# Order of products in a two-layer trunk: joint and third products by sixteens, and the end of the convolution

## The chip, the cores and the metric

The kernel runs on one core of a Trainium2 chip. Its time is the device time of one execution in microseconds, as the median of three runs. Times of parts come from one profiled execution of the kernel before.

## The reference

Two layers over 256 tokens of width 1024, in float32. Each layer is a half-step feed-forward block (SwiGLU, hidden width 2816), a token mixer, and another half-step feed-forward block, with RMS norms ahead of and behind each. The first layer's mixer is a convolution module, the second's a gated linear recurrence (HGRN2).

```python
def swiglu_ffn(x, w_in, w_out):
    gate, up = jnp.split(x @ w_in, 2, axis=-1)
    return (jax.nn.silu(gate) * up) @ w_out

def conformer_conv_module(x, w_in, b_in, w_dw, b_dw, ln_g, ln_b, w_out, b_out):
    a, gate = jnp.split(x @ w_in + b_in, 2, axis=-1)
    h = a * jax.nn.sigmoid(gate)
    h = lax.conv_general_dilated(  # 31 taps, causal, each channel by itself
        ...
    h = jax.nn.silu(layer_norm(h, ln_g, ln_b))
    return h @ w_out + b_out

for layer in range(DEPTH):
    ...
    x = x + 0.5 * rms_norm(h, g[1])
    hn = rms_norm(x, g[2])
    ...
```

## The kernel before

**Three products for one.** Float32 values are split into a high part (a cast to float32r, on ScalarE, L136) and the rest (a subtraction on VectorE, L137); `split` does both. A product of two such values is the sum of three: high by high, high by rest, rest by high. `mm3` (L140 to L142) issues the three.

**Tokens.** The 256 tokens are two tiles t = 0, 1 of 128. `xhl` holds the transposed input of the current block for both tiles, high and rest side by side.

**Feed-forward blocks.** There are four, each with 11 chunks of 256 hidden columns. Chunk 0 is done by tiles (`up`, `turn`), chunks 1 to 10 by `up_both(c, b)` for b = 0, 1, each of which calls `channels` once: 20 calls a block, 80 in all. `channels` computes 128 gate channels and 128 up channels for all tokens. A part (gate in a PSUM bank of the pool `mm`, up in one of `tr`, two banks in each pool) is eight joint products, the weight's high part by high and rest of `xhl` together (512 columns, L331), then eight third products, the weight's rest by the high part (256 columns, L333). A copy of the cross half and an add (L336, L337) read the bank. Behind two calls of `up_both` come the products of `down` of the chunk before (L140 to L142 into `acc`).

**The convolution, `conv_mixer`.** The channels lie in four chunks c of 256, so there are eight pairs (t, c). `gate(t, c)` projects (`project`, L291 to L295), adds the bias, and splits the gated value into `glu`. `conv(t, c)` takes it through a discrete Fourier transform: 6 or 12 small products into `tr` (L140 to L142 there), a complex multiplication by the taps' spectrum on VectorE (L513 to L517), a split into `yh`, `yl` (`cc` in the trace), six products back into another `tr` bank, the bias (L526) and the statistics of the layer norm (L527). `norm(t)` combines the statistics, takes the power on GpSimd (L151, L155) and makes z (L536). `turn(t, z)` transposes z in two halves of four blocks (L546), applies gain and bias by block on ScalarE (L553), then sigmoid (L557), multiplication (L558) and split into `xhl`: by pairs of blocks in the first half, all four at once in the second. `expand` multiplies the result by the output weights `wo` (48 products a tile), and `post_norm` (L267 to L279) adds it to x. What is returned as `rest` is run by the next block, ahead of its own norms (`start`, `pre_norm`, whose transposes are L175).

**What sets the order.** The kernel is written in Tile. Its scheduler fills the engines' queues at build time: of the instructions that by its own estimate of times are ready, the one written first goes first. What is written earlier is thus preferred, not fixed. On the chip each engine runs its queue in that order. `behind(engine)` keeps what is written under it behind the last instruction written for that engine. Banks and buffers of a pool are given in the order of use. Weights come on SyncE's queue (`weight`, L127) and are split as they land.

The convolution's written order is gate and conv for (0,0), (1,0), (0,1), (1,1), (0,2), (0,3); norm(0); gate and conv (1,2); gate(1,3); turn(0); conv(1,3); loads of rows and of `wo`; norm(1) and turn(1); expand(0) and post_norm(0).

Of the kernel before, what the change touches and what calls it, by code (L numbers as in the profile page):

```python
# [11 lines left out]
AF = mybir.ActivationFunctionType  # L12
ALU = mybir.AluOpType
# [27 lines left out]
def trunk_kernel(  # L41
# [39 lines left out]
    def acc():  # L81
        return new(ps, [P, 512], F32, "acc", 4)

    def mm():
        return new(ps, [P, 512], F32, "mm", 2)

    def tr():
        return new(ps, [P, 512], F32, "tr", 2)
# [46 lines left out]
    def split(dst_h, dst_l, src):  # L135
        act.copy(dst_h, src)  # L136
        dve.tensor_tensor(dst_l, src, dst_h.bitcast(F32), op=ALU.subtract)  # L137
# [185 lines left out]

    def channels(ws, cols_, scales):
        res = wide("ga")
        for part, bank in enumerate((mm, tr)):
            o = bank()
            pair = o.rearrange("p (s t m) -> p s t m", s=2, m=P)
            block = lambda w, k: w[:, (k % 2) * 512 + cols_[part] : (k % 2) * 512 + cols_[part] + P]
            for k in range(KD):  # L330
                pe.matmul(pair, block(ws[k // 2][0], k), xhl[:, k], start=k == 0, stop=False)  # L331
            for k in range(KD):
                pe.matmul(pair[:, 0], block(ws[k // 2][1], k), xhl[:, k, 0],  # L333
                          start=False, stop=k == KD - 1)
            cross = narrow("e")
            act.copy(cross, o[:, SEQ:])  # L336
            dve.tensor_tensor(res[:, part * SEQ : (part + 1) * SEQ], o[:, :SEQ], cross, op=ALU.add)  # L337
        dve.tensor_tensor(res[:, :SEQ], res[:, :SEQ], scales, op=ALU.mult)
        return res
# [131 lines left out]
    def conv_mixer(layer, spectrum, before):  # L471
# [4 lines left out]
        xt = start(base, before)  # L476
        hc = [b4() for _ in range(NT)]
        stats = [new(sb, [P, 4, 6], F32, "stats", 2) for _ in range(NT)]
        glu = {}
        ws = {}  # L480

        def gate(t, c):
# [12 lines left out]
            split(hl[:, :CH], hl[:, CH:], h)  # L495
            glu[t, c] = hl

        def conv(t, c):
            sl = slice(c * CH, (c + 1) * CH)
            u = tr()  # L500
            srcs = [(glu[t, c], C_FWD)]
            if t > 0:
# [8 lines left out]
            m1, m2 = wide("ca"), wide("cb")  # L511
            y = m1
            dve.tensor_tensor(m1[:NH], u[:NH, :], wri, op=ALU.mult)  # L513
            dve.tensor_tensor(m2[:NH, :CH], u[:NH, :CH], wi, op=ALU.mult)
            dve.tensor_tensor(m2[:NH, CH:], u[:NH, CH:], wr, op=ALU.mult)
            dve.tensor_tensor(y[:NH, :CH], m1[:NH, :CH], m1[:NH, CH:], op=ALU.subtract)
            dve.tensor_tensor(y[:NH, CH:], m2[:NH, :CH], m2[:NH, CH:], op=ALU.add)  # L517
            yh, yl = wide("cc", F32R), wide("cc", F32R)
            split(yh[:NH], yl[:NH], y[:NH])
            v = tr()  # L520
            for part in range(2):
                cs = slice(C_INV + part * P, C_INV + (part + 1) * P)
# [6 lines left out]
        def norm(t):  # L529
            mv = tiny(2)  # L530
            dve.bn_aggr(mv, stats[t])
            rstd = rsqrt(mv[:, 1:2], 1.0, EPS)
            z = b4()
            for n in range(2):
                sl = slice(n * 512, (n + 1) * 512)
                dve.tensor_scalar(z[:, sl], hc[t][:, sl], mv[:, 0:1], rstd,  # L536
                                  op0=ALU.subtract, op1=ALU.mult)
            return z

        def turn(t, z):  # L540
            hi, lo = turned(t)
            for h in range(2):
                pt = tr()
                for j in range(4):
                    k = h * 4 + j
                    pe.transpose(pt[:, j * P : (j + 1) * P], z[:, k * P : (k + 1) * P], ident)  # L546
                y, s = hc[t][:, h * 512 : (h + 1) * 512], z[:, h * 512 : (h + 1) * 512]
                for j in range(4):
                    k = h * 4 + j
                    js = slice(j * P, (j + 1) * P)  # L550
                    g = gcol[:, G_LN + k : G_LN + k + 1]
                    b = gcol[:, G_LN + KD + k : G_LN + KD + k + 1]
                    act.activation(y[:, js], pt[:, js], AF.Identity, scale=g, bias=b)  # L553
                step = 256 if h == 0 else 512
                for a in range(0, 512, step):
                    bs = slice(a, a + step)
                    act.activation(s[:, bs], y[:, bs], AF.Sigmoid)  # L557
                    dve.tensor_tensor(y[:, bs], y[:, bs], s[:, bs], op=ALU.mult)  # L558
                    ks = slice((h * 512 + a) // P, (h * 512 + a + step) // P)
                    split(hi[:, ks], lo[:, ks], y[:, bs].rearrange("p (k m) -> p k m", m=P))  # L560
            return hi, lo

        for t, c in ((0, 0), (1, 0), (0, 1), (1, 1), (0, 2)):
            gate(t, c)
            conv(t, c)
        gate(0, 3)
        conv(0, 3)
        za = norm(0)
        gate(1, 2)
        conv(1, 2)  # L570
        gate(1, 3)
        sa = turn(0, za)
        conv(1, 3)
        b_out = row(V_BOUT)
        gain = row(V_POST + base)
        wo = [weight(True) for _ in range(8)]
        sbt = turn(1, norm(1))
        accs = [[acc(), acc()] for _ in range(NT)]
        expand(accs[0], blocks(*sa, KD), wo, True, True)
        post_norm(0, accs[0], gain, 1.0, b_out)  # L580

# [361 lines left out]
```

## Time and profile before

| | |
|---|---|
| median of 3 runs | 1009.26 us (1008.78 to 1009.34) |
| profiled execution | 1008.88 us |
| its span, first to last instruction | 1007.0 us |
| mean granted TensorE clock | 0.995 |
| TensorE busy | 992.5 us |
| VectorE busy | 749.7 us |
| ScalarE busy | 548.6 us |

A row of a timeline is: start, duration, engine, line, operation, output<-inputs by the program's names, shapes, count; in square brackets idle time of the engine before it and what ended it. Products are pipelined, so durations overlap: what a product costs is the distance from its start to the next start. [...]

### The profile page before, as it was taken

The page shows a single profiled execution, that of the slowest core. Times are in us where ns is not written, and L with a number is a line of the kernel's source. Part 1 is how long each engine was busy: PE and PEld are TensorE (multiplying, and loading weights), DVE is VectorE, ACT ScalarE, POOL GpSimd, SP SyncE. Part 2 cuts the span into 40 slices and gives each one's busy share as a digit, 9 for nine tenths or more (in the row PEclk, how much of TensorE's full clock was granted, in tenths as well). Part 3 has the DMA queues.
Part 4 walks back from the last instruction along what each step waited for, and adds up shares of the span by engine and source line. Part 5 has one row for each costly group of instructions (what it writes and reads, how often), then busy time and mean ns, then how long its engine had stood idle before and what let it go on. Part 6 is the DMA issues. An engine that isn't in the chain of part 4 may idle for free.

```text
span 1007.0 us, 14787 instructions
## 1 busy us (share of the span) xinstructions
PE 992.5 (99%) x5412; PEld 854.8 (85%) x5412; DVE 749.7 (74%) x1274; ACT 548.6 (54%) x1000; POOL 53.6 (5%) x93
## 2 busy tenths in 40 slices
PE   9999999999899999999999999999999999999997
PEld 7888888888778888888888888889998888888886
DVE  6877667799887776767776767687788596767673
ACT  6656545764485555455755554584143385555541
POOL 1000000010021000000200000030001120000000
PEclk9999999999899999999999999999999999999999
DMA  7885555642527564646465646465232555555541
GB/s 250 273 279 181 187 198 172 236 179 104 181 96 235 180 219 161 222 160 221 168 198 178 210 166 223 167 208 179 82 126 93 179 195 181 189 187 199 178 147 42
DMA packets 50952, 182.06 MB, mean 181 GB/s; under 512 B 6048, under 2 KB 6176, under 8 KB 50880
## 3 DMA queue, kind: packets, MB, share of 16 engines
q1 hardware_dynamic: 50736, 181.09, 53.4%
q8 instruction: 42, 0.69, 0.3%
q14 instruction: 30, 0.25, 0.1%
q10 hardware_dynamic: 144, 0.03, 0.0%
HBM read 180.06 MB, written 1.05 MB: 180 GB/s over the span
## 4 chain that ended last, share of the span: by engine, by line
PE 94%; DVE 2%; ACT 1%; DMA 1%; POOL 1%; issue 0%; DVEq 0%; POOLq 0%; SPq 0%; ACTq 0%
PE tr L331 14%; PE mm L331 14%; PE acc L141 9%; PE acc L140 9%; PE acc L142 9%; PE tr L333 7%; PE mm L333 7%; PE mm L291 4%; PE mm L292 4%; PE mm L295 4%; PE tr L654 2%; PE mm L351 2%; PE mm L352 2%; PE mm L350 2%; DMA raw<-wts 1%; PE tr L175 1%
## 5 line engine op out<-in xcount | busy, mean ns | idle before, releaser
L137 DVE TENSOR_TENSOR wl<-raw,wh 128x1024 fp32r<-128x1024 f32 (+1 forms) x386 | 399.9, 1059 | 89.1 <-ACT wh L136 65.0
L136 ACT CAST wh<-raw 128x1024 fp32r<-128x1024 f32 (+1 forms) x386 | 340.4, 921 | 124.7 <-DMA raw<-wts 72.3
L331 PE MATMUL mm<-xt,wh 128*128 128x512 f32 x640 | 161.6, 393 | 0.5 <-ACT wh L136 0.5
L331 PE MATMUL tr<-xt,wh 128*128 128x512 f32 x640 | 160.7, 392 | 0.0
L140 PE MATMUL acc<-wh,b 128*128 128x512 f32 x352 | 138.0, 392 | 0.0
L141 PE MATMUL acc<-wl,b 128*128 128x512 f32 x352 | 137.4, 390 | 0.0
L331 PEld LDWEIGHTS mm<-xt,wh 128*128 128x128 f32 x640 | 116.9, 188 | 24.1 <-ACT wh L136 1.3
L142 PE MATMUL acc<-wh,b 128*128 128x512 f32 x352 | 137.0, 389 | 0.0
L331 PEld LDWEIGHTS tr<-xt,wh 128*128 128x128 f32 x640 | 115.0, 189 | 20.7
L333 PEld LDWEIGHTS mm<-xt,wl 128*128 128x128 f32 x640 | 87.5, 190 | 6.7 <-DVE wl L137 0.4
L333 PEld LDWEIGHTS tr<-xt,wl 128*128 128x128 f32 x640 | 87.3, 190 | 6.2
L333 PE MATMUL mm<-xt,wl 128*128 128x256 f32 x640 | 90.0, 282 | 0.2 <-DVE wl L137 0.2
L333 PE MATMUL tr<-xt,wl 128*128 128x256 f32 x640 | 89.2, 282 | 0.0
L136 ACT CAST b<-e 128x256 fp32r<-128x256 f32 x80 | 32.5, 406 | 95.8 <-DVE e L412 95.8
L142 PEld LDWEIGHTS acc<-wh,b 128*128 128x128 f32 x352 | 66.1, 188 | 14.1
L140 PEld LDWEIGHTS acc<-wh,b 128*128 128x128 f32 x352 | 66.2, 188 | 12.6
L141 PEld LDWEIGHTS acc<-wl,b 128*128 128x128 f32 x352 | 66.2, 188 | 12.2
L336 ACT COPY e<-tr 128x256 f32<-128x256 f32 x80 | 29.4, 368 | 85.1 <-PE tr L333 85.1
L337 DVE TENSOR_TENSOR ga<-tr,e 128x256 f32<-128x256 f32 x80 | 33.7, 421 | 55.6 <-ACT e L336 55.6
L291 PE MATMUL mm<-wh,xt 128*128 128x512 f32 x176 | 70.0, 398 | 0.0
L292 PE MATMUL mm<-wl,xt 128*128 128x512 f32 x176 | 69.2, 393 | 0.0
L336 ACT COPY e<-mm 128x256 f32<-128x256 f32 x80 | 29.7, 371 | 49.0 <-PE mm L333 48.8
(180 smaller groups left out, 1251.9 us busy)
## 6 DMA issues: line engine op xcount, KB each, us to landing
raw<-wts SPq DMA_DIRECT2D x328, 512.0 KB, 4.8
b<-rows SPq DMA_DIRECT2D x10, 512.0 KB, 6.5
b<-x_turned SPq DMA_DIRECT2D x4, 256.0 KB, 6.3
x<-x_in SPq DMA_DIRECT2D x2, 512.0 KB, 8.4
out_dram<-x SPq DMA_DIRECT2D x4, 256.0 KB, 2.0
b<-dft SPq DMA_DIRECT2D x1, 371.0 KB, 4.8
ca<-masks SPq DMA_DIRECT2D x1, 192.0 KB, 4.5
b<-w_dw SPq DMA_DIRECT2D x1, 128.0 KB, 4.9
```

The source lines that it names most:

```text
L136: act.copy(dst_h, src)
L137: dve.tensor_tensor(dst_l, src, dst_h.bitcast(F32), op=ALU.subtract)
L140: pe.matmul(o, lh, rh, start=first, stop=False)
L141: pe.matmul(o, lh, rl, start=False, stop=False)
L142: pe.matmul(o, ll, rh, start=False, stop=last)
L291: pe.matmul(o, hi[:, k], wh[:, sl], start=k == 0, stop=False)
L292: pe.matmul(o, hi[:, k], wl[:, sl], start=False, stop=False)
L295: pe.matmul(o, a, w, start=False, stop=h == 1 and n == 3)
L331: pe.matmul(pair, block(ws[k // 2][0], k), xhl[:, k], start=k == 0, stop=False)
L333: pe.matmul(pair[:, 0], block(ws[k // 2][1], k), xhl[:, k, 0], start=False, stop=k == KD - 1)
L336: act.copy(cross, o[:, SEQ:])
L337: dve.tensor_tensor(res[:, part * SEQ : (part + 1) * SEQ], o[:, :SEQ], cross, op=ALU.add)
```

## The change

In `channels` the four groups of eight products are issued in another order: joint products of gate, joint of up, third of gate, third of up. Both banks are taken at the start, and both are read at the end.

In `conv_mixer`, `conv` is cut in two, `spectral` (up to the split) and `back` (the six products back, bias, statistics). For (1,2), `back` is written behind gate(1,3) and turn(0). Of the two multiplications by half of the spectrum's swapped parts one of 512 columns is made, which reads the spectrum with its halves exchanged. In `turn`, gain and bias, sigmoid, multiplication and split go by pairs of blocks in both halves. turn(1) gets the bank `accs[1][0]` as `spare`: behind its last transposes 16 products of the identity by itself are written into it, whose result nobody reads. The accumulators are taken ahead of turn(1) for that.

```diff
--- before.py
+++ after.py
@@ -323,15 +323,18 @@
 
     def channels(ws, cols_, scales):
         res = wide("ga")
-        for part, bank in enumerate((mm, tr)):
-            o = bank()
+        banks = [mm(), tr()]
+        for o, col in zip(banks, cols_):
             pair = o.rearrange("p (s t m) -> p s t m", s=2, m=P)
-            block = lambda w, k: w[:, (k % 2) * 512 + cols_[part] : (k % 2) * 512 + cols_[part] + P]
             for k in range(KD):
-                pe.matmul(pair, block(ws[k // 2][0], k), xhl[:, k], start=k == 0, stop=False)
+                wh = ws[k // 2][0][:, (k % 2) * 512 + col : (k % 2) * 512 + col + P]
+                pe.matmul(pair, wh, xhl[:, k], start=k == 0, stop=False)
+        for o, col in zip(banks, cols_):
+            pair = o.rearrange("p (s t m) -> p s t m", s=2, m=P)
             for k in range(KD):
-                pe.matmul(pair[:, 0], block(ws[k // 2][1], k), xhl[:, k, 0],
-                          start=False, stop=k == KD - 1)
+                wl = ws[k // 2][1][:, (k % 2) * 512 + col : (k % 2) * 512 + col + P]
+                pe.matmul(pair[:, 0], wl, xhl[:, k, 0], start=False, stop=k == KD - 1)
+        for part, o in enumerate(banks):
             cross = narrow("e")
             act.copy(cross, o[:, SEQ:])
             dve.tensor_tensor(res[:, part * SEQ : (part + 1) * SEQ], o[:, :SEQ], cross, op=ALU.add)
@@ -476,7 +479,7 @@
         xt = start(base, before)
         hc = [b4() for _ in range(NT)]
         stats = [new(sb, [P, 4, 6], F32, "stats", 2) for _ in range(NT)]
-        glu = {}
+        glu, prod = {}, {}
         ws = {}
 
         def gate(t, c):
@@ -495,8 +498,7 @@
             split(hl[:, :CH], hl[:, CH:], h)
             glu[t, c] = hl
 
-        def conv(t, c):
-            sl = slice(c * CH, (c + 1) * CH)
+        def spectral(t, c):
             u = tr()
             srcs = [(glu[t, c], C_FWD)]
             if t > 0:
@@ -511,12 +513,18 @@
             m1, m2 = wide("ca"), wide("cb")
             y = m1
             dve.tensor_tensor(m1[:NH], u[:NH, :], wri, op=ALU.mult)
-            dve.tensor_tensor(m2[:NH, :CH], u[:NH, :CH], wi, op=ALU.mult)
-            dve.tensor_tensor(m2[:NH, CH:], u[:NH, CH:], wr, op=ALU.mult)
+            dve.tensor_tensor(m2[:NH].rearrange("p (s n) -> p s n", s=2),
+                              u[:NH].rearrange("p (s n) -> p s n", s=2),
+                              wri.rearrange("p (s n) -> p s n", s=2)[:, ::-1, :], op=ALU.mult)
             dve.tensor_tensor(y[:NH, :CH], m1[:NH, :CH], m1[:NH, CH:], op=ALU.subtract)
             dve.tensor_tensor(y[:NH, CH:], m2[:NH, :CH], m2[:NH, CH:], op=ALU.add)
             yh, yl = wide("cc", F32R), wide("cc", F32R)
             split(yh[:NH], yl[:NH], y[:NH])
+            prod[t, c] = yh, yl
+
+        def back(t, c):
+            yh, yl = prod.pop((t, c))
+            sl = slice(c * CH, (c + 1) * CH)
             v = tr()
             for part in range(2):
                 cs = slice(C_INV + part * P, C_INV + (part + 1) * P)
@@ -537,45 +545,49 @@
                                   op0=ALU.subtract, op1=ALU.mult)
             return z
 
-        def turn(t, z):
+        def turn(t, z, spare=None):
             hi, lo = turned(t)
             for h in range(2):
                 pt = tr()
                 for j in range(4):
                     k = h * 4 + j
                     pe.transpose(pt[:, j * P : (j + 1) * P], z[:, k * P : (k + 1) * P], ident)
+                if spare is not None and h == 1:
+                    with behind(pe):
+                        for j in range(16):
+                            pe.matmul(spare[:, j % 4 * P : (j % 4 + 1) * P], ident, ident, start=True, stop=True)
                 y, s = hc[t][:, h * 512 : (h + 1) * 512], z[:, h * 512 : (h + 1) * 512]
-                for j in range(4):
-                    k = h * 4 + j
-                    js = slice(j * P, (j + 1) * P)
-                    g = gcol[:, G_LN + k : G_LN + k + 1]
-                    b = gcol[:, G_LN + KD + k : G_LN + KD + k + 1]
-                    act.activation(y[:, js], pt[:, js], AF.Identity, scale=g, bias=b)
-                step = 256 if h == 0 else 512
-                for a in range(0, 512, step):
-                    bs = slice(a, a + step)
+                for a in range(0, 512, 256):
+                    bs = slice(a, a + 256)
+                    ks = slice((h * 512 + a) // P, (h * 512 + a + 256) // P)
+                    for j in range(a // P, a // P + 2):
+                        k = h * 4 + j
+                        js = slice(j * P, (j + 1) * P)
+                        g = gcol[:, G_LN + k : G_LN + k + 1]
+                        b = gcol[:, G_LN + KD + k : G_LN + KD + k + 1]
+                        act.activation(y[:, js], pt[:, js], AF.Identity, scale=g, bias=b)
                     act.activation(s[:, bs], y[:, bs], AF.Sigmoid)
                     dve.tensor_tensor(y[:, bs], y[:, bs], s[:, bs], op=ALU.mult)
-                    ks = slice((h * 512 + a) // P, (h * 512 + a + step) // P)
                     split(hi[:, ks], lo[:, ks], y[:, bs].rearrange("p (k m) -> p k m", m=P))
             return hi, lo
 
-        for t, c in ((0, 0), (1, 0), (0, 1), (1, 1), (0, 2)):
+        for t, c in ((0, 0), (1, 0), (0, 1), (1, 1), (0, 2), (0, 3)):
             gate(t, c)
-            conv(t, c)
-        gate(0, 3)
-        conv(0, 3)
+            spectral(t, c)
+            back(t, c)
         za = norm(0)
         gate(1, 2)
-        conv(1, 2)
+        spectral(1, 2)
         gate(1, 3)
         sa = turn(0, za)
-        conv(1, 3)
+        back(1, 2)
+        spectral(1, 3)
+        back(1, 3)
         b_out = row(V_BOUT)
         gain = row(V_POST + base)
         wo = [weight(True) for _ in range(8)]
-        sbt = turn(1, norm(1))
         accs = [[acc(), acc()] for _ in range(NT)]
+        sbt = turn(1, norm(1), accs[1][0])
         expand(accs[0], blocks(*sa, KD), wo, True, True)
         post_norm(0, accs[0], gain, 1.0, b_out)
```

## Rows read from the trace of the kernel before

**Rows 1.** The page's first part: busy time and share of the span of TensorE.
```profile
PE 992.5 (99%) x5412; PEld 854.8 (85%) x5412; DVE 749.7 (74%) x1274; ACT 548.6 (54%) x1000; POOL 53.6 (5%) x93
```

**Rows 2.** Windows: stretch, length, busy PE, PEld, DVE, ACT, POOL, clock, DMA.
```profile
256.00:281.00 25.00, 20.80 (x95) 16.80 (x94) 20.10 (x44) 14.25 (x35) 0.74 (x2) 0.86 0.43 158
...
300.00:1000.00 700.00, 700.00 (x3916) 609.51 (x3915) 509.43 (x824) 366.97 (x638) 35.20 (x57) 1.00 0.53 176
```

**Rows 3.** TensorE's waits: sum, count, longest.
```profile
PE tr L140 <- ACT cc L136: 2.7, 1, 2.7
...
PE tr L175 <- DVE x L279: 1.2, 2, 0.6
```

**Rows 4.** Timeline of TensorE in a chunk of the second feed-forward block.
```profile
323.11 1.98 PE L331 MATMUL mm<-xt,wh 128*128 128x512 f32 x8
324.92 1.12 PE L333 MATMUL mm<-xt,wl 128*128 128x256 f32 x8
325.88 2.00 PE L331 MATMUL tr<-xt,wh 128*128 128x512 f32 x8
327.72 1.12 PE L333 MATMUL tr<-xt,wl 128*128 128x256 f32 x8
328.67 2.00 PE L331 MATMUL mm<-xt,wh 128*128 128x512 f32 x8
```

**Rows 5.** Timeline of TensorE at the convolution's end.
```profile
255.44 1.08 PE L295 MATMUL mm<-wh,xt 128*128 128x512 f32 x4
259.24 0.39 PE L140 MATMUL tr<-cc,b 81*128 81x256 f32 x1 [2.72 <-ACT cc L136]
259.46 0.66 PE L546 MATMUL tr<-ident,b 128*128 128x128 f32 x4
...
276.67 1.11 PE L546 MATMUL tr<-ident,b 128*128 128x128 f32 x8 [0.29 <-DVE b L536]
277.54 0.47 PE L140 MATMUL acc<-wh,xt 128*128 128x512 f32 x1
...
278.77 0.40 PE L142 MATMUL acc<-wh,xt 128*128 128x512 f32 x1
280.18 0.50 PE L140 MATMUL acc<-wh,xt 128*128 128x512 f32 x1 [1.01 <-ACT xt L136]
```

**Rows 6.** Windows of 2 us at the convolution's end.
```profile
258.00:260.00 2.00, 0.77 (x5) 0.59 (x5) 2.00 (x6) 1.33 (x3) 0.00 (x0) 0.97 0.61 248
260.00:262.00 2.00, 1.82 (x8) 1.43 (x8) 1.41 (x5) 1.85 (x6) 0.00 (x0) 0.50 0.00 0
...
266.00:268.00 2.00, 2.00 (x9) 1.60 (x8) 2.00 (x6) 1.74 (x4) 0.00 (x0) 0.82 0.51 168
```

**Rows 7.** The page's groups: busy us, mean ns, idle before.
```profile
L337 DVE TENSOR_TENSOR ga<-tr,e 128x256 f32<-128x256 f32 x80 | 33.7, 421 | 55.6 <-ACT e L336 55.6
```

**Rows 8.** Timeline of TensorE early in the first feed-forward block.
```profile
41.27 0.50 PE L333 MATMUL mm<-xt,wl 128*128 128x256 f32 x2 [0.23 <-DVE wl L137]
```

**Rows 9.** Timeline of VectorE at the convolution's end.
```profile
254.31 1.01 DVE L536 TENSOR_SCALAR b<-b,tiny,tiny 128x512 f32<-128x512 f32 x2 [0.71 <-POOL tiny L155]
...
255.83 0.68 DVE L513 TENSOR_TENSOR ca<-tr,b 81x512 f32<-81x512 f32 x1
256.43 0.41 DVE L514 TENSOR_TENSOR cb<-tr,b 81x256 f32<-81x256 f32 x1
256.76 0.41 DVE L515 TENSOR_TENSOR cb<-tr,b 81x256 f32<-81x256 f32 x1
...
276.07 1.00 DVE L536 TENSOR_SCALAR b<-b,tiny,tiny 128x512 f32<-128x512 f32 x2 [0.95 <-POOL tiny L155]
```

**Rows 10.** Waits from 256 to 286: VectorE's for TensorE.
```profile
DVE b L526 <- PE tr L142: 1.9, 2, 1.3
...
DVE ca L513 <- PE tr L142: 0.6, 1, 0.6
```

**Rows 11.** Timeline of TensorE at the kernel's start.
```profile
1.50 5.49 PE L202 MATMUL tr<-ident 128*128 128x128 f32 x24 [1.50 <-POOL ident masks.py:199]
```

## The prediction

> **What bounds the kernel now.** I read the page's first part, then the windows by stage, TensorE's waits, and the timelines of the two places that the change touches. TensorE is busy for 992.5 of 1007.0 us and no other engine is near that [rows 1]. In the windows the 700 us after the convolution have no idle time at all on TensorE at a granted clock of 1.00, while the 25 us at the convolution's end (256 to 281) have 20.80 busy and a clock of 0.86 [rows 2]. So time can go only in two ways: make the stream of products itself shorter, or close what is lost at the convolution's end. The list of waits agrees: the longest is 2.7 us, a product `tr<-cc` that waits for a split on ScalarE; two waits of transposes for `x`, up to 0.6 each, stand a little behind [rows 3].
>
> **The lost time, added up.** Product starts in the timeline [rows 5] give it. The last four products of gate(1,3) start at 255.44, 0.23 apart, so the next could start at 256.35; it starts at 259.24: 2.9 lost. Later pauses are 0.29 and 1.01 [rows 5] and one of the two of 0.6 [rows 3], each with 0.15 or so around it for the pipeline to refill (from 278.77 to 280.18 are 1.41, a product's spacing of 0.23 and the wait of 1.01 leave 0.17): 2.4 together. [...] Two us by the missing shares is 2 x (0.03 + 0.5 + 0.5 + 0.5 + 0.18) = 3.4 us. Sum: 2.9 + 2.4 + 3.4 = 8.7 us. It is all that the convolution part can win.
>
> **Part 1, `channels`.** It removes and adds no product: 8 joint (512 columns), 8 third (256), 8 joint, 8 third become 16 joint, 16 third. The price lies at the seams. Joint eights that follow other 512-column products take 1.81 us (323.11 to 324.92); those that follow thirds take 1.84 (325.88 to 327.72) [rows 4]. Thirds take 0.95 to 0.96 an eight, 0.12 each. The change takes one seam third-to-joint out of each call: 0.03 us. It also takes one joint-to-third seam out, which gains nothing or gives back up to 0.01, the rounding of the rows. There are 80 calls (x80) [rows 7]. So 80 x 0.02 = 1.6 us less; by rounding between 0.8 and 2.8. The third products now come 1.8 us after the last joint of their own bank, so `wl` has that much longer: the wait of 0.23 at 41.27, 0.4 with the refill [rows 8], should go; I take 0.3. Joint products need all four `wh` as soon as before, so waits for `wh` stay.
>
> What it moves: both banks now fill almost together, and the `mm` bank is read 2.8 us later. The work on each bank ends with an add of 0.42 [rows 7] behind a copy of like size; the same bank is asked for two calls later, and a call lasts 5.56 us (323.11 to 328.67) [rows 4]. That is the cover, and it is wide; without it each of 80 calls would wait. At the end of a feed-forward block the chain after the last third product still ends with the `tr` half, so no change there.
>
> **Part 2, the order at the convolution's end.** TensorE takes instructions in queue order, and that order isn't the written one: products of expand(0), written last, stand on both sides of turn(1)'s transposes (`acc<-wh,xt` goes on at 277.54) [rows 5]. Written order works as a priority among what the scheduler deems ready. Before, the inverse products of conv(1,2) have priority over turn(0); the first one waits until 259.24 for `yh`, and turn(0)'s transposes, whose `z` was done at 255.32 [rows 9], wait behind it until 259.46. The reason that `yh` is late is on VectorE: it idles 0.71 for GpSimd's power, then does `z`, and only from 255.83 the products of conv(1,2) [rows 9]. Told ahead of back(1,2), the transposes can start at about 256.4, 3.0 us earlier (their bank was last used by conv(0,3)). So turn(0)'s activations and splits, and with them expand(0), come up to 3 us earlier.
>
> What is late next? (a) TensorE between 256.4 and 260 has only eight transposes (0.9 us) and six inverse products (0.7): I take 2.0 us of pause as left, bounds 0.5 and 2.9. (b) VectorE: from 255.83 to 277.07, the end of z(1), it idles 1.9 (two waits for the inverse products), 0.6 and 0.95 = 3.45 [rows 9, 10], so some 17.8 us of work lie ahead of z(1), the splits of `wo` among it. z(1) can't end before 273.6 unless splits go behind it; 0.95 for GpSimd remains; so 274.6, which is 2.5 us earlier. TensorE has, until turn(1), 48 products of expand(0) at 0.227, 24 small ones of the convolution at 0.12 and 8 transposes at 0.11 [rows 4, 5]: 10.9 + 2.9 + 0.9 = 14.7 us, so with the pause of 2.0 from 256.35 to about 273. The two fit: TensorE is through with expand(0) shortly before z(1) is there. (c) the combined multiplication: two of 256 lie 0.33 apart and one of 512 takes 0.60 to the next [rows 9], so 0.06 less in each of 8 blocks, only the last on the path. Two halves instead of one 512 in turn's second part cost the same 0.06 or so for each multiplication and split, and let the first half go on sooner. I count all of (c) as nothing.
>
> [...]
>
> **Part 3, identity products.** [...] Sixteen make 32 instructions: 3.5 us by the near row in form and clock, 7.3 by the other, which is the bound; I take 3.5. They stand behind the last transposes of turn(1) and ahead of whatever of expand(0) isn't issued yet. The pause they are to fill is, before, from 277.54 to 280.18, 2.6 us, of which six products of expand(0) take 1.4 and 1.01 is seen as idle. If expand(0) is through by then, 2.6 us of 3.5 are covered; if not, they delay it. Either way I charge all 3.5 against the removal of the whole pause. They write `accs[1][0]`, which nobody needs before expand(1).
>
> **Sum of parts 2 and 3.** 8.7 are lost now; after: 2.0 pause at 256 to 260, 3.5 identity products in place of the last pause, 0.7 for the smaller waits that stay (z(1), `x`). Left 6.2, so 2.5 less. This takes the clock as held. With part 1: 2.5 + 1.6 + 0.3 = 4.4 us. The profiled execution took 1008.88 (its span 1007.0 and 1.88 around it), so 1004.5; the median of the runs is 0.38 above it, so **1004.9 us**. Bounds of the unknown costs around it: 1.5 either way for the pause, 1.0 for the seams, so about 1002.4 to 1007.4.
>
> **Rivals.**
> *The clock falls anyway.* For it: it fell about where the pause before 259.24 ended, and in the change the same stretch holds only short work, mostly transposes. Against it: the transposes and the inverse products break the pause, where before it was whole [rows 5]. Price: the 3.4 us stay, and 1004.9 + 3.4 = 1008.3, no measurable change. [...]
> *Slower: the identity products run with real work queued behind them at half clock.* It decides if the clock is still down when turn(1) is transposed. Then they take 7 us rather than 3.5, on top of the case above: 1008.3 + 3.5 = 1011.8. Against it: the stretch at half clock ended before 268 [rows 6], well ahead of 276.67 [rows 5].
> *It doesn't do what it says.* The scheduler places by its own estimate; if back(1,2) still goes ahead, part 2 gives nothing and the products cost 3.5 less the 1.2 of the pause: 1009.26 - 1.9 + 2.3 = 1009.7.
> *More than forecast.* Both pauses shrink to 0.5 and the identity products fit into a pause that the chain through z(1) leaves anyway: 1.5 and 1.8 more, 1001.6.
>
> **How the numbers follow.** Forecast 0.55, clock falls 0.15, slower 0.08, order unchanged 0.08, more 0.14. A change of 0.2%, 2.0 us, is about what a measurement of this kernel can tell from none. Faster by more: the forecast and the larger gain, 0.69, and a little of the clock's case, in all 0.70; within: 0.20; slower: 0.10. The range, 1001.2 to 1009.2, takes in all but the slower case and the edges of the others.
>
> **What would show it.** In the changed trace: joint sixteens of about 3.63 to 3.66 us and third sixteens of 1.91; turn(0)'s first transposes at about 256.4 rather than 259.46 and ahead of the inverse products; a clock of 1.00 from 256 to 281; 32 identity instructions 0.11 apart, with at most 0.3 us of pause behind them; the transposes of `x` for the next block (285.1 before) some 2.5 us earlier in that stage. I am wrong if the seams don't shrink, if the clock is 0.50 again around 260, or if the identity products stand ahead of many products of expand(0).

## The result, and the profile after

The changed kernel is slower. Its median is 1021.09 us (1020.51 to 1021.63), that of the kernel before, run beside it, 1009.30 (1008.78 to 1010.73): a ratio of 1.0113, 95% interval 1.0100 to 1.0126, or 11.8 us more. The forecast was 1004.9, the range 1001.2 to 1009.2; sign and range are wrong. The profiled execution of the changed kernel took 1020.51 us, its span is 1018.7.

The windows of the kernel after say where (columns as in [rows 2]):

```profile
256.00:281.00 25.00, 13.24 (x70) 11.61 (x69) 19.36 (x44) 14.65 (x39) 0.74 (x2) 0.66 0.48 165
...
306.00:1006.00 700.00, 699.16 (x3919) 609.42 (x3918) 507.12 (x826) 372.67 (x649) 35.13 (x60) 1.00 0.52 175
```

The 700 us behind the convolution are all but as full as before, 699.16 us of work against 700.00 [rows 2]. In the 25 us at its end TensorE worked 13.24 us where it had worked 20.80 [rows 2], at a clock of 0.66 for 0.86. The timeline of TensorE in that stretch, kernel after; the rows with brackets are pieces of work that begin behind a pause:

```profile
256.94 1.04 PE L554 MATMUL tr<-ident,b 128*128 128x128 f32 x8
260.67 0.39 PE L140 MATMUL tr<-cc,b 81*128 81x256 f32 x1 [2.69 <-ACT b L568]
...
262.98 0.50 PE L140 MATMUL tr<-lg,b 128*81 128x256 f32 x1 [1.34 <-ACT b L568]
...
269.46 0.58 PE L140 MATMUL tr<-cc,b 81*128 81x256 f32 x1 [3.63 <-ACT cc L136]
...
275.58 1.94 PE L554 MATMUL tr<-ident,b 128*128 128x128 f32 x8 [3.53 <-DVE b L544]
277.31 4.65 PE L558 MATMUL acc<-ident 128*128 128x128 f32 x32
281.71 0.48 PE L140 MATMUL acc<-wh,xt 128*128 128x512 f32 x1
...
296.44 1.38 PE L175 MATMUL tr<-ident,x 128*128 128x128 f32 x8 [0.18 <-DVE x L279]
```

The first line is the early start of turn(0) as forecast: its eight transposes in one piece at 256.94, where their first half had come at 259.46 [rows 5]. What is missing is `acc<-wh,xt`: before, 42 of the 48 products of expand(0) ran ahead of turn(1)'s transposes; now not one does. The first stands at 281.71, behind the identity products. With nothing to run beside the convolution's chain TensorE waits 2.69, 1.34, 3.63 and 3.53 us. The clock is down with it (windows of 4 us, the clock is the third number from the end):

```profile
260.00:264.00 4.00, 1.99 (x11) 1.79 (x12) 4.00 (x12) 4.00 (x13) 0.00 (x0) 0.77 0.39 144
...
268.00:272.00 4.00, 1.97 (x6) 1.43 (x6) 4.00 (x8) 0.62 (x1) 0.00 (x0) 0.50 0.46 148
...
276.00:280.00 4.00, 4.00 (x24) 4.00 (x23) 1.19 (x3) 3.30 (x10) 0.00 (x0) 0.60 0.36 139
```

It fell to 0.50 at about 262.2 and rose at 279.2, 17 us against 6.8 before.

**The account.** From turn(1)'s transposes to those of `x` it is 296.44 - 275.58 = 20.86 us after. Before, from 276.67 [rows 5] to this row of the same timeline, it was 8.45:

```profile
285.12 0.66 PE L175 MATMUL tr<-ident,x 128*128 128x128 f32 x4 [0.57 <-DVE x L279]
```

Between them stand 63 products of the expansions rather than 24: 39 x 0.227 = 8.9. The identity products take 281.71 - 277.31 = 4.4, the transposes at half clock 277.31 - 275.58 = 1.73 rather than 0.87, so 0.9 more. The pause of 1.01 with its refill is gone (-1.2) and the wait for `x` is 0.4 shorter. Together 12.6; measured 12.4. turn(1) came 1.1 us earlier (0.8 of it from before the convolution), which leaves 11.3 at the transposes of `x`. The rest is small: +0.9 from there to the second feed-forward block, where 33 products of the expansions are left rather than 30 (0.7), -0.4 in each of the three blocks that follow, +0.6 between two of them. That makes the 11.7 by which the span grew.

**Part 1 did what it said, block by block.** Timeline of a chunk, kernel after:

```profile
335.31 1.98 PE L331 MATMUL mm<-xt,wh 128*128 128x512 f32 x8
337.12 1.98 PE L331 MATMUL tr<-xt,wh 128*128 128x512 f32 x8
338.93 1.11 PE L336 MATMUL mm<-xt,wl 128*128 128x256 f32 x8
339.88 1.12 PE L336 MATMUL tr<-xt,wl 128*128 128x256 f32 x8
340.84 0.40 PE L331 MATMUL mm<-xt,wh 128*128 128x512 f32 x1
```

Sixteen joint products take 338.93 - 335.31 = 3.62, sixteen third products 1.91, a call 5.53 where it was 5.56 [rows 4]. The first joint product of a block and the first product behind its last call, before and then after:

```profile
491.14 0.48 PE L331 MATMUL mm<-xt,wh 128*128 128x512 f32 x1
...
649.85 0.40 PE L140 MATMUL acc<-wh,b 128*128 128x512 f32 x1
```
```profile
503.61 0.48 PE L331 MATMUL mm<-xt,wh 128*128 128x512 f32 x1
...
661.93 0.40 PE L140 MATMUL acc<-wh,b 128*128 128x512 f32 x1
```

158.71 us became 158.32. The wait for `wl` of [rows 8] is gone.

### The profile page after: what moved, and what is told of

Read it like the earlier page. It is cut to its first block, busy times and chain, and to the rows that moved or that the text cites. A ratio compares the mean times of both kernels' runs of the same rounds, so it can differ in the third digit from the quotient of the medians.

```text
span 1018.7 us, 14830 instructions
## 1 busy us (share of the span) xinstructions
PE 996.0 (98%) x5444; PEld 859.6 (84%) x5444; DVE 746.6 (73%) x1270; ACT 552.4 (54%) x1004; POOL 49.1 (5%) x93
## 4 chain that ended last, share of the span: by engine, by line
PE 93%; DVE 3%; ACT 2%; DMA 1%; POOL 1%; issue 0%; DVEq 0%; POOLq 0%; SPq 0%; ACTq 0%
PE mm L331 14%; PE tr L331 14%; PE acc L141 9%; PE acc L140 9%; PE acc L142 9%; PE mm L336 7%; PE tr L336 7%; PE mm L295 4%; PE mm L292 4%; PE mm L291 4%; PE tr L666 2%; PE mm L354 2%; PE mm L355 2%; PE mm L353 2%; DVE wl L137 1%; DMA raw<-wts 1%
## 5 line engine op out<-in xcount | busy, mean ns | idle before, releaser
L331 PE MATMUL tr<-xt,wh 128*128 128x512 f32 x640 | 158.6, 390 | 0.0
L331 PEld LDWEIGHTS tr<-xt,wh 128*128 128x128 f32 x640 | 119.8, 188 | 25.3 <-DVE ga L340 0.4
L336 PEld LDWEIGHTS tr<-xt,wl 128*128 128x128 f32 x640 | 82.8, 192 | 0.3
L140 PEld LDWEIGHTS acc<-wh,b 128*128 128x128 f32 x352 | 66.2, 188 | 12.6
L340 DVE TENSOR_TENSOR ga<-mm,e 128x256 f32<-128x256 f32 x80 | 33.6, 420 | 52.4 <-ACT e L339 52.4
L413 ACT ACTIVATE e<-ga 128x256 f32<-128x256 f32 x80 | 33.5, 419 | 57.9 <-DVE ga L341 56.1
```

The lines of the kernel that those rows point to most:

```text
L140: pe.matmul(o, lh, rh, start=first, stop=False)
L331: pe.matmul(pair, wh, xhl[:, k], start=k == 0, stop=False)
L336: pe.matmul(pair[:, 0], wl, xhl[:, k, 0], start=False, stop=k == KD - 1)
L413: act.activation(h, gu[:, :SEQ], AF.Sigmoid)
```

## The experiments

Theory: the identity products, as the first in the kernel's text to write a bank of `acc`, decide the order in which the banks of that pool are handed out; the scheduler then can't queue expand(0), written behind them in the same pool, before them, and they stand behind turn(1). Rivals: the time of the identity products themselves; the new order of turn(0) and back(1,2); the clock. "Told" stands for written in the kernel's text. Ratios are against the kernel before, run in the same group.

| kernel | median us (runs) | before | ratio, 95% interval |
|---|---|---|---|
| e1_no_identity | 1008.70 (11) | 1009.82 | 0.9984, 0.9976 to 0.9993 |
| e2_channels_only | 1010.27 (11) | 1009.82 | 1.0003, 0.9995 to 1.0012 |
| e3_identity_only | 1024.07 (4) | 1009.82 | 1.0131, 1.0116 to 1.0146 |
| e4_identity_in_mm | 1010.16 (12) | 1009.82 | 1.0003, 0.9993 to 1.0013 |
| e6_one_identity | 1019.05 (4) | 1009.95 | 1.0085, 1.0072 to 1.0098 |
| e7_expand_told_first | 1009.37 (10) | 1009.95 | 0.9996, 0.9987 to 1.0005 |
| e11_turn_in_mm | 1007.06 (5) | 1009.95 | 0.9965, 0.9953 to 0.9977 |
| e11b_turn_in_mm, the same again | 1007.13 (9) | 1009.67 | 0.9973, 0.9963 to 0.9982 |
| e13_identity_first_pause | 1007.49 (8) | 1009.95 | 0.9977, 0.9967 to 0.9988 |
| e10_back_early | 1009.60 (11) | 1010.16 | 0.9997, 0.9988 to 1.0005 |
| e12_turn_in_mm_expand_first | 1008.23 (11) | 1010.16 | 0.9984, 0.9975 to 0.9993 |
| e16_old_channels_e12 | 1008.40 (11) | 1010.16 | 0.9984, 0.9975 to 0.9993 |
| e14_identity_first_pause_mm | 1007.49 (7) | 1010.16 | 0.9973, 0.9962 to 0.9983 |
| e18_joint_third_by_twos | 1007.73 (11) | 1009.67 | 0.9981, 0.9972 to 0.9990 |
| e15_old_channels_e11 | 1007.63 (11) | 1009.67 | 0.9979, 0.9970 to 0.9987 |

### Who makes it slow: the identity products, and by their bank

**e1** leaves the identity products out of the changed kernel; the accumulators are still taken ahead of turn(1).

```diff
-        sbt = turn(1, norm(1), accs[1][0])
+        sbt = turn(1, norm(1))
```

> The changed kernel (1021.1) without the sixteen identity products, all else kept. Theory A (the identities take the first bank of the pool acc, which the scheduler hands out in order of first writing in the text, so the 48 products of expand(0) can't be queued ahead of them): expand(0) is back ahead of turn(1), 44 of its 48 products; 1005 to 1007. Theory B (the new order of back(1,2) and turn(0) is itself the loss, through the banks of tr and ScalarE): 1015 or more. Theory C (only the time of the 32 identity instructions at half clock, 4.7 us, and nothing else): 1021.1 - 4.7 = 1016.4.

**e3** puts them alone into the kernel before, by the same lines in its `turn`.

```diff
-        sbt = turn(1, norm(1))
         accs = [[acc(), acc()] for _ in range(NT)]
+        sbt = turn(1, norm(1), accs[1][0])
```

> The kernel before with the identity products alone, into accs[1][0], and the accumulators taken ahead of turn(1). Theory A: expand(0) falls behind turn(1) here too, 42 products of 0.227 (9.5 us) lose their place beside the chain through VectorE and the clock falls for longer: 1019 to 1023. Theory B: only the products' own time, 3.5 less the pause of 1.2: 1011.6. Theory C: 1009.3 + 4.7 = 1014.

**e4** is the changed kernel with the same 32 instructions in a bank of another pool.

```diff
-        sbt = turn(1, norm(1), accs[1][0])
+        sbt = turn(1, norm(1), mm())
```

> The changed kernel with the sixteen identity products written into a bank of the pool mm rather than accs[1][0]; same number, same place behind the last transposes of turn(1). Theory A: expand(0) comes back ahead of turn(1) (44 of 48), the identities cost at most 3.5 less what of the last pause they fill: 1006 to 1009. Theories B and C: as the changed kernel, 1020 to 1022.

e1 is 1.1 us faster than the kernel before where the changed kernel is 11.8 slower, e3 is 14.3 slower, and e4, with every identity product still there and still behind turn(1)'s transposes, is level with it. In e1 44 of the 48 products of expand(0) are back ahead of turn(1), in e4 too; in e3 none is, although its turn(0), its back(1,2) and its `channels` are those of before. TensorE in e3, behind a pause that the kernel before has as 0.29 [rows 5]:

```profile
276.32 1.97 PE L546 MATMUL tr<-ident,b 128*128 128x128 f32 x8 [3.43 <-DVE b L536]
278.09 5.52 PE L550 MATMUL acc<-ident 128*128 128x128 f32 x32
283.36 0.48 PE L140 MATMUL acc<-wh,xt 128*128 128x512 f32 x1
```

In e4 the identity products stand at the same place, and expand(0) goes on around them:

```profile
276.48 0.39 PE L141 MATMUL acc<-wl,xt 128*128 128x512 f32 x1
277.23 1.06 PE L554 MATMUL tr<-ident,b 128*128 128x128 f32 x8 [0.36 <-DVE b L544]
278.13 3.74 PE L558 MATMUL mm<-ident 128*128 128x128 f32 x32
281.62 0.48 PE L142 MATMUL acc<-wh,xt 128*128 128x512 f32 x1
```

So the new order at the convolution's end isn't the cause, and neither is the identity products' own time in the main: it is the bank.

**e6** keeps one identity product of sixteen, in the same bank, and **e7** keeps all and the bank, but tells expand(0) ahead of turn(1), so that it is the first to write `acc`.

```diff
-                        for j in range(16):
+                        for j in range(1):
```

> The changed kernel with one identity product instead of sixteen, still written into accs[1][0] behind turn(1)'s last transposes. Theory A (the order of the acc banks): 30 instructions less, which took about 4.1 us of the stretch of 4.4 in the changed kernel, and everything else stays: 1021.1 - 4.1 = 1017; expand(0) still wholly behind turn(1). If the number of identities were the cause: near the kernel without them, 1009 to 1010.

```diff
-        sbt = turn(1, norm(1), accs[1][0])
         expand(accs[0], blocks(*sa, KD), wo, True, True)
+        sbt = turn(1, norm(1), accs[1][0])
```

> The changed kernel with expand(0) written ahead of turn(1), sixteen identities into accs[1][0] as in the change. Theory A: with expand(0) the first to write into the pool acc its products are free to go early, 48 of 48 ahead of turn(1); the identities cost what they don't fill of the last pause (1.83 without them): 1008 to 1011. Theories that blame the bank accs[1][0] itself or the identities as such: 1018 or more.

One product holds back as much as sixteen. e6, whose transposes of turn(1) come at 276.41:

```profile
278.14 0.63 PE L558 MATMUL acc<-ident 128*128 128x128 f32 x2
278.43 0.77 PE L140 MATMUL acc<-wh,xt 128*128 128x512 f32 x1
```

Thirty instructions fewer gave 2.0 us between the medians (2.7 with each against the kernel before beside it) of the 11.8: expand(0) still begins behind turn(1), and now its first products run at half clock, which rose at 280.4. In e7 all 48 products stand ahead, and the time is that of the kernel before:

```profile
274.63 1.03 PE L554 MATMUL tr<-ident,b 128*128 128x128 f32 x8
275.50 3.74 PE L558 MATMUL acc<-ident 128*128 128x128 f32 x32
279.00 0.48 PE L140 MATMUL acc<-wh,xt 128*128 128x512 f32 x1
```

Here the forecast for turn(1), 274.6, comes true, and TensorE reaches it without a wait. The cause of the slowdown is settled by e6 and e7 together with e3 and e4. That it is the order of first use within the pool is how the scheduler was read; what the runs show is that the same instructions hold expand(0) back in a bank of `acc` when told before it, and neither in `mm` nor when told behind it. Being first is not enough by itself: in e14 below the first writer of `acc` is early on TensorE too (258.12), and 44 products of expand(0) stand ahead of turn(1).

### What the early transposes are worth

TensorE in e1, where turn(0)'s transposes stand ahead of the products of back(1,2):

```profile
257.17 1.03 PE L554 MATMUL tr<-ident,b 128*128 128x128 f32 x8
260.88 0.39 PE L140 MATMUL tr<-cc,b 81*128 81x256 f32 x1 [2.68 <-ACT b L568]
...
276.01 1.06 PE L554 MATMUL tr<-ident,b 128*128 128x128 f32 x8 [0.36 <-DVE b L544]
...
279.84 0.49 PE L140 MATMUL acc<-wh,xt 128*128 128x512 f32 x1 [1.83 <-ACT xt L136]
```

The pause of 2.72 [rows 5] was not broken but moved behind the transposes, and what ends it is new: no longer the split of `yh`, but the activation that empties the `tr` bank (L568). The pool has two `tr` banks; turn(0)'s halves hold both, and the inverse products ask for the third.

**e10** is e1 with back(1,2) told where it stood.

```diff
         spectral(1, 2)
+        back(1, 2)
         gate(1, 3)
         sa = turn(0, za)
-        back(1, 2)
```

> The changed kernel without identities and with back(1,2) written where it was, right behind spectral(1,2). If writing it later is worth what the prediction charged to the early transposes (2.5 us): 1008.7 + 2.5 = 1011.2. If the later place only swaps one wait on TensorE (2.72 for yh before) for another (2.68 for a bank of tr): 1008.5 to 1009.5.

0.9997 against e1's 0.9984: late telling is worth about 1 us, and the two intervals overlap. In its trace the order is that of before again, with the pause 2.89. The clocks listed with the runs differ as well: in the mean 0.9962 in e10's eleven and 0.9974 in e1's, a difference which by estimate is worth 1.2 of 1008 us (a share of 0.0012), as much as what is put down to late telling. Whether late telling brought the higher clock isn't shown.

**e11** takes the bank off the path: turn's transposes go into `mm`.

```diff
-                pt = tr()
+                pt = mm()
```

This stands on top of e1.

> The changed kernel without identities, with turn's transposes in banks of mm rather than tr. Without identities the first inverse product of (1,2) waits 2.68 us, for ScalarE to read turn(0)'s transposes out of the two tr banks; yh is there at 259.2, 1.6 us before. If that bank is what holds TensorE: 1 to 1.6 us less, and the clock falls for a shorter time or not at all, up to 1.7 more: 1005.5 to 1007.5. If the chain through VectorE to z(1) is what counts: 1008.7 as without the move.

> The same kernel as e11_turn_in_mm, as the partner of the next one on the same chip: 1007.1 there; 1006 to 1008.

It has the lowest medians of all, ratios 0.9965 and 0.9973 (e14 below has 0.9973 too): 2.5 to 2.9 us faster than the kernel before. The list of TensorE's waits at the convolution's end, second trace of this kernel:

```profile
PE acc L140 <- ACT xt L136: 1.6, 1, 1.6
PE mm L554 <- DVE ga L491: 0.7, 1, 0.7
...
PE tr L140 <- ACT cc L136: 0.4, 1, 0.4
PE tr L140 <- ACT lg L136: 0.3, 1, 0.3
```

The wait for L568 is gone; 0.7, 0.4 and 0.3 are left of 2.7. So the pause could shrink below the 2.0 that the prediction took, but only with the transposes out of `tr`.

**e12** is e11 with expand(0) told ahead of turn(1), the move of e7.

```diff
-        sbt = turn(1, norm(1))
         expand(accs[0], blocks(*sa, KD), wo, True, True)
+        sbt = turn(1, norm(1))
```

> The changed kernel without identities, turn's transposes in banks of mm, expand(0) written ahead of turn(1). Against 1007.1 with the same order of writing as the change: x is done earlier as expand(0) is through earlier, but the last pause stays open (1.6 us): 1006 to 1008.

No better than e11. The two products of expand(0) that stand behind turn(1) in e11 are ahead of it here, and turn(1) comes at 274.04 (274.95 and 275.52 in e11's traces), but the `xt` that the next expansion needs is no earlier: its first product starts at 278.25 (278.15 and 278.72), and the wait for `xt` is 3.1 us where e11 has 1.6.

### What the sixteens are worth

**e2** is the kernel before with the new `channels` alone. **e15** is e11 and **e16** is e12, each with the old `channels`: the diff's first part, forwards in e2, backwards in the other two.

```diff
-        for part, bank in enumerate((mm, tr)):
-            o = bank()
+        banks = [mm(), tr()]
+        for o, col in zip(banks, cols_):
...
```

> The kernel before with the new order of joint and third products alone. If the seam third-to-joint costs 0.03 us and a second eight of thirds 0.01 more: 80 x 0.02 = 1.6, and 0.3 of a wait for wl, so 1009.3 - 1.9 = 1007.4. If reading both banks at the end costs anything in each call: 1009.3 or more.

> The kernel e11_turn_in_mm with channels as in the kernel before. If seams reach the total: 1.5 us above its partner. If not, within 0.5 of it, as in the pair e12 and e16.

> The kernel e12_turn_in_mm_expand_first of this same group of runs, with channels as in the kernel before (8 joint, 8 third, 8 joint, 8 third). At the convolution's end the queues of the two differ in the place of six products only. If the seams are worth 20 x 0.019 us in each of four feed-forward blocks: 1.5 us above e12. If reading both banks at the end gives it back elsewhere in the blocks: as e12, within 0.5.

e2 shows no gain (+0.45 us); e11b is 0.5 us faster than e15, e12 0.2 faster than e16: all within their intervals. Yet the third and fourth feed-forward blocks, from the first joint product to the first product behind the last call, take 158.70 to 158.74 in every kernel with the old order and 158.32 to 158.38 in every one with the new. Two places where it comes back can be seen. One is the transposes of `x`, which wait 1.2 us in all in the kernel before [rows 3] and 1.6 to 3.5 in the traces of e1, e2, e4, e7, e11 and e12, at the ends of the blocks too; but e15, with the old order, has 2.2, so they don't belong to the seams alone. The other is a bank. VectorE in e11's second trace, as the second feed-forward block begins:

```profile
309.45 2.51 DVE L137 TENSOR_TENSOR wl<-raw,wh 128x1024 fp32r<-128x1024 f32 x2 [1.01 <-ACT wh L136]
311.87 0.42 DVE L340 TENSOR_TENSOR ga<-mm,e 128x256 f32<-128x256 f32 x1
312.21 0.42 DVE L340 TENSOR_TENSOR ga<-tr,e 128x256 f32<-128x256 f32 x1
```

The adds that free both banks stand behind two weight splits, and a joint product waits 0.7 us for them (0.4 in e2, 0.9 in e11). e3 and e16, with the old order, have that wait too (0.5, 0.4), so it isn't the new order's alone either. How the sum of -1.1 us in three blocks comes to nothing in e2 stays open; one trace of each kernel can't part it from what differs between executions.

The clocks listed with the runs give a lead. In the mean they are 0.9946 in e2's eleven and 0.9961 in the 29 of the kernel before beside them; 0.9966 in e12 and 0.9975 in e16; 0.9976 in e11b and 0.9980 in e15: lower with the new order in all three pairs. By estimate e2's difference (0.0014 before rounding) is worth 1.4 of its 1008 us, of the size of what the blocks won; in the other pairs it is 0.8 and 0.4. Why the clock should be lower, and where in a run, isn't shown.

**e18** tests the price of a seam: in the kernel before, joint and third products go by twos, so a call has four times the seams.

```diff
+            for h in range(0, KD, 2):
+                for k in (h, h + 1):
+                    pe.matmul(pair, block(ws[k // 2][0], k), xhl[:, k], start=k == 0, stop=False)
+                for k in (h, h + 1):
+                    pe.matmul(pair[:, 0], block(ws[k // 2][1], k), xhl[:, k, 0],
+                              start=False, stop=k == KD - 1)
```

> The kernel before with joint and third products alternating by twos in channels: seven more places in each call where thirds end and joints begin or the other way round, on each bank, and the convolution's end queued on TensorE as in the kernel before. In the trace of before the first two joints after thirds take 0.015 more than later ones and the first third after joints 0.007 less: six more seams a call of 0.008, 0.05 us a call, 20 calls a block: a block about 0.9 us longer. If seams reach the total: 1009.8 + 3.6 = 1013.4. If what a block gains or loses is given back at the waits between blocks: 1009.5 to 1011.

```profile
404.81 0.61 PE L332 MATMUL mm<-xt,wh 128*128 128x512 f32 x2
405.26 0.40 PE L334 MATMUL mm<-xt,wl 128*128 128x256 f32 x2
405.50 0.63 PE L332 MATMUL mm<-xt,wh 128*128 128x512 f32 x2
405.96 0.39 PE L334 MATMUL mm<-xt,wl 128*128 128x256 f32 x2
```

Two joint products take 405.96 - 405.50 = 0.46, as in an eight behind thirds (1.84 / 4) and not 0.45 as in one behind joint products [rows 4]. The thirds are a little cheaper: 406.19 - 405.96 = 0.23 for the second pair (406.19 is the next joint's start), 0.22 to 0.24 and in the mean 0.23 for the eight pairs of this call, where two in an eight take 0.24 [rows 4]. Four times the seams should have cost; the block takes 158.51, less than the 158.71 of eights, and the kernel is 0.19% faster than before. A fixed price for a seam is disproved. Where the 1.9 us come from is open: three blocks give 0.6.

### Identity products in the first pause

**e13** is e1 with eight identity products behind turn(0)'s transposes, in a bank of `mm`; **e14** is e11 with the same eight, in a bank of `acc`.

```diff
+                        spare = mm()
-                        for j in range(16):
+                        for j in range(8):
...
-        sa = turn(0, za)
+        sa = turn(0, za, True)
```

> The changed kernel with eight identity products behind turn(0)'s transposes, in a bank of mm, and none behind turn(1). They are 16 instructions, about 1.8 us, in a pause of 2.7 us. If the clock is held by them: the 3.4 us at 0.50 after the pause are gone, 1.7 us less than the 1008.7 without identities: 1007.0. If the clock falls anyway, or the chain through VectorE sets the end: 1008.7; if they delay back(1,2): 1009.5.

> The changed kernel with turn's transposes in mm and eight identities behind those of turn(0), in a bank of acc that is free then, none behind turn(1). The pause there is 0.9 + 0.5 us in pieces when the transposes are in mm, less than the 16 instructions take (1.8), so they delay back(1,2) by up to 0.5; if they hold the clock that the same kernel without them lost for 3.4 us (1.7 us of time): 1006 to 1007. If the clock falls on chance alone: 1007 to 1008.

The windows from 260 to 264 in e13, e14, e4 and e7, in that order:

```profile
260.00:264.00 4.00, 3.15 (x18) 2.65 (x19) 4.00 (x11) 4.00 (x14) 0.00 (x0) 1.00 0.40 143
```
```profile
260.00:264.00 4.00, 4.00 (x28) 3.64 (x27) 4.00 (x12) 4.00 (x12) 0.00 (x0) 1.00 0.40 137
```
```profile
260.00:264.00 4.00, 3.31 (x11) 2.93 (x12) 4.00 (x12) 4.00 (x13) 0.00 (x0) 0.55 0.41 146
```
```profile
260.00:264.00 4.00, 3.37 (x20) 2.86 (x21) 4.00 (x12) 4.00 (x13) 0.00 (x0) 1.00 0.38 138
```

In e13 and e14 the clock held in this stretch; in e13 it fell later, at 278.7, for 3.4 us. It buys little: 1007.49 in both; e13 is some 1.3 us more below the kernel before than e1, and e14 is no better than e11. And e7 held 1.00 too, with nothing in its pause of 2.66 us, so one profile of each doesn't show that the identity products did it. Over all their runs the listed clock averages 0.9982 and 0.9984, against 0.9974 in e1 and 0.9976 to 0.9978 in e11: it leans that way, by less than single runs of one kernel differ (0.995 to 0.999 in e1).

## Why the prediction was wrong

**The step that failed** is in Part 3: "They write `accs[1][0]`, which nobody needs before expand(1)." It asked who needs the bank on the chip. The bank mattered at build time, as the first of its pool in the text. The fact stood in the description of the kernel: banks are given in the order of use. And the diff moves `accs` up for this one argument. The sentence ahead of it, that the identity products stand "ahead of whatever of expand(0) isn't issued yet", was right; that this would be all 48 products was not asked, since Part 2 had already put them in front of turn(1). The runs e3, e4 and e7 show this step alone carrying 11 to 14 us: e3 is 14.3 us above the kernel before, and the kernel after is 10.9 above e4 and 11.7 above e7, by the medians. The prediction's own sign for being wrong, "if the identity products stand ahead of many products of expand(0)", is what the trace shows; so is, from 262.2 on, "if the clock is 0.50 again around 260".

**The price of the identity products.** 3.5 us was forecast for 32 instructions, by the spacing of transposes, with 7.3 as the bound, by the spacing of 0.23 at the kernel's start [rows 11]. No run shows the 7.3, nor what set that spacing; the window of before over that stretch reads a clock of 1.00:

```profile
0.00:7.00 7.00, 5.49 (x24) 5.20 (x24) 0.88 (x2) 2.83 (x5) 0.88 (x8) 1.00 0.70 195
```

At a clock of 1.00 they take 3.5 (e7, 275.50 to 279.00); after took 4.4, because the first of them ran at 0.50, until 279.2, and in e3, at 0.50 until 281.8, it was 5.3. In a bank that holds nothing back (e4) the kernel is 1.5 us slower than without them (e1).

**The early transposes.** The move was right in place (256.4 forecast; 256.94 in the kernel after, 257.17 in e1). The pause left was sized 2.0, bounds 0.5 to 2.9, and is 2.69: inside the bounds, but by luck, since what ends it is not `yh` but a bank of `tr`. Who else holds `tr` would have given it: turn(0) uses both banks, and in e11, with turn(0) out of them, that wait is gone. The forecast of 274.6 for turn(1) holds where the clock stays up (e7); at 3.4 us of half clock it is 276.01 (e1), at 6.8 it is 277.23 (e4). (In the kernel after it is 275.58, with none of expand(0) ahead of it.) Parts 2 and 3 were to give 2.5 us; e1, with part 2 and the seams and without part 3, gives 1.1.

**The clock.** The 3.4 us counted as lost before come from five windows of 2 us, three in [rows 6] and the two between them:

```profile
262.00:264.00 2.00, 2.00 (x11) 2.00 (x10) 2.00 (x5) 1.91 (x6) 0.00 (x0) 0.50 0.69 262
264.00:266.00 2.00, 2.00 (x9) 1.85 (x8) 1.43 (x4) 2.00 (x6) 0.00 (x0) 0.50 0.32 102
```

"Forecast" took the clock as held; in the kernel after it fell for 17 us. The rival for that, at 3.4 us, assumed the old length of the stretch. The length goes with expand(0) missing: in the kernels without it ahead of turn(1) the clock is at 0.50 in this stretch for 17.1 us (after) and 20.5 (e3), and in e6 still from 276 to 280.4; in those with it for 0 (e7) to 6.8 (e4).

**The seams.** Forecast 1.6 us for 80 calls, 0.02 each. The call shows 0.03, the block 0.37 to 0.39 for 20 calls, so the row was read rightly; the step that failed is the sum, which let each block's gain pass to the end of the kernel, where e2 shows none (+0.45 us). The cover named for the banks, "it is wide", was two calls' length and not what stands in VectorE's queue: behind two weight splits of 1.2 us it gave way once, by 0.2 to 0.9 us, in seven of the traces with the new order (and in two with the old).

**The rivals.** The slower one, identity products "with real work queued behind them at half clock", had the right place and 1011.8 as its price. It decides "if the clock is still down when turn(1) is transposed", which it was. What it lacked was the work displaced: 39 products of 0.227, 8.9 us, more than twice its 3.5. "It doesn't do what it says" didn't happen: the scheduler did queue turn(0) ahead of back(1,2).

**What makes the clock fall.** In after, e1 and e4 a pause of 2.68 to 2.69 us that followed eight transposes ended at 260.67, 260.88 and 260.69, and by the windows the clock fell at 262.2, 261.5 and 260.4; in e7, behind the same work and a pause of 2.66, it did not fall. All four have both the pause and the transposes, so no run here tells what the one or the other does. That transposes and inverse products, by breaking the pause, would hold the clock was the author's argument; it isn't shown either.

## What to carry to other kernels

Filler work isn't free because nobody reads its result: ask which pool its bank is from and who is the next to be given one, since the first writer in the text, where it comes late on its engine, can hold back every later user of that pool, here all 48 products of expand(0) (after, e3 and e6). When an instruction is told earlier, compare the whole queue of its engine before and after, not the instruction alone: the loss here was in 42 products that the diff doesn't touch. A gain that is certain in each block isn't yet one of the kernel: e2 has it in three blocks and not in its time, so measure the part alone.

## What the runs showed of the chip

The granted clock around a like pause, with the same work ahead of it, differed between traces: 0.50 for 3.4 us in e1, for 6.8 us in e4 and not at all in e7, with pauses of 2.68, 2.68 and 2.66 us. Within one kernel it differed too: e1's eleven runs list mean clocks of 0.995 to 0.999. A pair of third products (256 columns) took 0.23 us in the mean right behind joint products (one call of e18) and 0.24 within an eight [rows 4], a pair of joints 0.46 behind thirds and 0.45 behind joints; in e18, which alternates by twos, this cost nothing (158.51 us a block rather than 158.71).
